# The seven-product FFN kernel: its zone moved by 64 bytes, and the A12 product made fourth of seven

## The chip, the cores and the metric

The kernel runs on one core of one Trainium2 chip. The metric is device time in microseconds (us); the median of the runs is the kernel's time. TensorE is called PE, ScalarE ACT, VectorE DVE, GpSimd POOL and SyncE SP, as in the profile.

## What is computed

A trunk of two layers over 256 rows of 2048 float32 values. Layer 0 has gated linear attention as its mixer, layer 1 attention over 64 selected keys. After each mixer comes a SwiGLU of width 5632, and this is the part that the change touches:

```python
def swiglu(h, w1, w3, w2):
    return (jax.nn.silu(h @ w1) * (h @ w3)) @ w2

for i in range(DEPTH):                      # DEPTH = 2, D_MODEL = 2048, SEQ = 256
    h = rmsnorm(x, norm_mix[i])
    x = x + (gla_mixer(h, ...) if i % 2 == 0 else dsa_mixer(h, ...))
    x = x + swiglu(rmsnorm(x, norm_ffn[i]), ffn_w1[i], ffn_w3[i], ffn_w2[i])
return rmsnorm(x, norm_final)
```

Every weight is read once from HBM in float32.

## The kernel before

**One product.** Weights come in as tiles `raw` of 128 x 4 x 512 float32 (1 MB), loaded by SP. ACT copies a tile to `wh` in the format that PE multiplies fast (L136, in the function `split_w`), and DVE subtracts to get the rest, `wl` (L137). The activations are split in the same way into a high and a low tile. Three matmuls (high by `wh`, high by `wl`, low by `wh`) make one product at nearly full accuracy. The moving operand is always the weight tile, 512 columns; the stationary operand is a 128 x 128 block of the activations. There are four `raw` buffers and three each of `wh` and `wl`.

**The FFN.** `ffn` goes through 11 blocks of 512 hidden columns. Blocks 0, 1, 3, 5, 7 and 9 run `plain`: for w1 and for w3 four groups of 24 matmuls (L464). Blocks 2, 4, 6, 8 and 10 run `pair`, which gets both products of a block, for two halves of the rows, with seven half-sized products instead of eight, by sums of activations (the forms A11, F5, F3, F6, F7, A12, N22 of the normed x) and of weights. A product in `pair` is 24 matmuls (L394) on two chunks of weights. There are two layers, so 10 pairs, with 7 products each, and 12 plain blocks.

**The sums of weights.** `va` and `vb` are the upper halves of w1 and w3, two tiles each. A11 uses `va`, then DVE adds `vb` to it (`plus`, L406). F5 uses the sum, and each of its chunks, once split, gets the lower half of w3 added by a DMA on POOL's queue that accumulates in SBUF (`plus_dma`, L409). F3 uses the lower half of w3, `vc`, loaded through `raw` (L381), and DVE adds it to `vb`. F6 uses `va`, and then a second pair of accumulating DMAs adds the lower half of w1. F7 uses `vb`, A12 the lower half of w1, `vd`, loaded through `raw`, and N22 uses `va`.

**The pieces.** `pair` and `plain` are generators. At each `yield`, `ffn` runs one piece of `pieces`: the down product of two finished blocks, 24 matmuls with one `raw` tile (L483, L490 to L492). The stationary operand there is a tile `g` of finished hidden values. A pair has eight `yield`s, and two blocks make eight pieces, so that pieces and products alternate. `side` holds transposes and their evacuation (`split_t`, L216 to L219), of which a step is taken by `tick` in the middle of products and pieces.

**The order.** The order on each engine follows the program's, with loads moved ahead where their buffer is free: SP issues the loads of the next pair's `va` while the plain block before it runs. On each queue instructions run in order, and one that waits holds up those behind it.

**Where tiles lie.** Pools are allocated one after the other along a partition. `res` holds x and the four tiles `g`, `wp` holds `raw`, `wh` and `wl`, `cm` and `sm` small things. Behind them lies a zone that four pools use in turn: `gp` and `dp` for the mixers (with the normed activations `hh` and `hl`, stationary operands of `gemm`, L202 to L204), `fz0` and `fz1` for the FFNs (with the forms `fh` and `fl`, and `v0`, `v1`, `v2`, `s1`, `y`, `w`). Two tiles named `pad` are never used; they move what is allocated after them. `x`, `g`, `raw`, `wh`, `wl` and the zone begin at these bytes of a partition in the program as built: 3072, 19456, 52224, 84992, 109568 and 140736.

Of the kernel before, what the change touches and what calls it, by code (L numbers as in the profile page):

```python
# [12 lines left out]
F32 = mybir.dt.float32  # L13
# [6 lines left out]
P = 128  # L20
# [35 lines left out]
def trunk(  # L56
# [7 lines left out]
    nc = tc.nc  # L64
# [5 lines left out]
    sm = ctx.enter_context(tc.tile_pool(name="sm", bufs=2))  # L70
# [24 lines left out]
    cols = cst.tile([P, 72], F32, name="cols")  # L95


    sm.tile([P, 24], F32, tag="pad", bufs=1, name="pad")

    def gains(c0, srcs):  # L100

# [14 lines left out]
    def tick():  # L116

        while side:
            try:
                return next(side[0])  # L120
            except StopIteration:
                side.popleft()
# [9 lines left out]
    def split_w(raw, pool=wp):  # L132

        wh = pool.tile([P, 4, NB], F32R, tag="wh", bufs=3 if pool is wp else 1, name="wh")
        wl = pool.tile([P, 4, NB], F32R, tag="wl", bufs=3 if pool is wp else 1, name="wl")
        nc.scalar.copy(wh, raw)  # L136
        nc.vector.tensor_sub(wl, raw, wh.bitcast(F32))  # L137
        return wh, wl
# [230 lines left out]
    def pair(nrm, wa, wb, c0, turn, done):  # L369

        def src(w, j, c):
            r = j * 1024 + c * 512
            return w[r:r + 512, c0:c0 + NB].rearrange("(k p) n -> p k n", p=P)

        def load(w, j, homes):
            o = []
            for c, (pool, tag, bufs) in enumerate(homes):
                raw = pool.tile([P, 4, NB], F32, tag=tag, bufs=bufs, name=tag)  # L380
                nc.sync.dma_start(raw, src(w, j, c))  # L381
                o.append(raw)
            return o

        def product(acc, raws, form, start, stop, then=None):
            for c in range(2):
                wh, wl = split_w(raws[c])
                if then is not None:
                    then(c)
                hi, lo = nrm.forms[form]  # L390
                for j in range(4):
                    k = 4 * c + j
                    for i, (l_, r_) in enumerate(((hi, wh), (hi, wl), (lo, wh))):
                        nc.tensor.matmul(acc, l_[:, k, :], r_[:, j, :], start=start and k == i == 0,  # L394
                                         stop=stop and k == 7 and i == 2, skip_group_check=not start)
                    if j % 2:
                        tick()

        def bank():
            return acc_p.tile([P, NB], F32, tag="acc", name="acc")  # L400

        def sums(tag):
            return nrm.pool.tile([P, NB], F32, tag=tag, bufs=1, name=tag)

        def plus(dst, other):
            return lambda c: nc.vector.tensor_add(dst[c], dst[c], other[c])  # L406

        def plus_dma(dst, w, j):
            return lambda c: nc.gpsimd.dma_start(dst[c], src(w, j, c), accum_op=ALU.add)  # L409

        fz = nrm.pool
        stream = [(wp, "raw", RAW)] * 2
        homes = [((fz, "v0", 1), (fz, "v1", 1)), ((fz, "v2", 1), (res, "g3", 1))]
        va = load(wa, 0, homes[turn])
        vb = load(wb, 0, homes[1 - turn])
        b1 = bank()
        product(b1, va, "A11", True, True, plus(va, vb))
        s1 = sums("s1")
        nc.scalar.copy(s1, b1)
        yield  # L420
        b2 = bank()
        product(b2, va, "F5", True, True, plus_dma(va, wb, 1))
        y = sums("y")
        nc.vector.tensor_sub(y, b2, s1)
        yield
        vc = load(wb, 1, stream)
        product(b2, vc, "F3", False, True, plus(vb, vc))
        yield
        b3 = bank()
        product(b3, va, "F6", True, True, plus_dma(va, wa, 1))  # L430
        w = sums("w")
        nc.vector.tensor_sub(w, b3, s1)
        yield
        product(b3, vb, "F7", False, True)
        nc.vector.tensor_add(w, w, b2)
        nc.vector.tensor_add(y, y, b3)
        yield
        vd = load(wa, 1, stream)
        product(b1, vd, "A12", False, True)
        done("11", b1)  # L440
        done("12", w)
        yield
        product(b3, va, "N22", False, True)
        nc.vector.tensor_sub(s1, s1, b3)
        done("21", s1)
        done("22", y)
        yield
        yield

    def plain(nrm, ws, c0, done):  # L450
# [49 lines left out]
    def ffn(layer, nrm):  # L500
# [5 lines left out]
        for b in range(DFF // NB):  # L506
            us = [None] * NT

            def done(q, v):
                t = int(q[0]) - 1  # L510
                if q[1] == "1":
                    us[t] = cm.tile([P, NB], F32, tag="u", name="u")
                    nc.scalar.activation(us[t], v, AF.Silu, scale=sc["r"][:, t:t + 1])
                else:
                    nc.vector.scalar_tensor_tensor(us[t], us[t], sc["r"][:, t:t + 1], v, op0=ALU.mult, op1=ALU.mult)

            for slot, _ in enumerate(pair(nrm, w1, w3, b * NB, b // 2 % 2, done) if b in range(2, 11, 2) else plain(nrm, (w1, w3), b * NB, done)):
                if b == 0 and slot == 0:
                    flush()
                    r = nrm.rstd()  # L520
                    sc["r"] = r
                while down:
                    try:
                        next(down[0])
                        break
                    except StopIteration:
                        down.popleft()
            hi, lo = hi_lo(b % 3)
            side.append(split_t(us, hi, lo))
            parts.append((hi, lo, b * NB))  # L530
            if b % 2:
                down.append(pieces(w2, parts))
                parts = []
# [560 lines left out]
```

## Time and profile before

| | |
|---|---|
| median of 3 runs | 2283.49 us |
| lowest and highest | 2281.22 and 2284.84 us |
| the profiled execution's own time | 2283.89 us |
| its span | 2282.1 us |
| busy: PE, weight loads, DVE, ACT, POOL | 2254.4, 1856.3, 1499.3, 1127.5, 79.3 us |
| mean granted clock of PE | 0.998 |
| read from HBM | 464.43 MB, 204 GB/s over the span |

The span is the time from the first to the last instruction of the profiled execution. Matmuls overlap, and the end of each is modelled, so PE shows as busy nearly all the time; what a matmul costs is read from one start to the next. A row of the timeline gives the start, the duration, the engine, the line, the operation, output and inputs, and in brackets how long the engine was idle before it and what ended that.

### The profile page before, as it was taken

The page shows a single profiled execution, that of the slowest core. Times are in us where ns is not written, and L with a number is a line of the kernel's source. Part 1 is how long each engine was busy: PE and PEld are TensorE (multiplying, and loading weights), DVE is VectorE, ACT ScalarE, POOL GpSimd, SP SyncE. Part 2 cuts the span into 40 slices and gives each one's busy share as a digit, 9 for nine tenths or more (in the row PEclk, how much of TensorE's full clock was granted, in tenths as well). Part 3 has the DMA queues.
Part 4 walks back from the last instruction along what each step waited for, and adds up shares of the span by engine and source line. Part 5 has one row for each costly group of instructions (what it writes and reads, how often), then busy time and mean ns, then how long its engine had stood idle before and what let it go on. Part 6 is the DMA issues. An engine that isn't in the chain of part 4 may idle for free.

```text
span 2282.1 us, 25208 instructions
## 1 busy us (share of the span) xinstructions
PE 2254.4 (99%) x10343; PEld 1856.3 (81%) x10343; DVE 1499.3 (66%) x1254; ACT 1127.5 (49%) x1026; POOL 79.3 (3%) x131
## 2 busy tenths in 40 slices
PE   9999999999999999999999999999999999999998
PEld 7888888887888888887888888888888788888886
DVE  6546456577676867776655755556675867777676
ACT  5545355444454545545544544455454454545454
POOL 0000000000000000000100000000000000000000
PEclk9999999999999999999999999999999999999999
DMA  8555465759495876857554555457496786949593
GB/s 286 168 171 188 127 233 187 237 160 302 147 299 199 216 263 184 289 159 218 173 182 148 184 166 166 165 186 240 147 277 234 193 273 174 296 146 305 166 239 111
DMA packets 242098, 468.18 MB, mean 205 GB/s; under 512 B 7816, under 2 KB 20448, under 8 KB 241856
## 3 DMA queue, kind: packets, MB, share of 16 engines
q1 hardware_dynamic: 219856, 423.33, 54.4%
q0 software_dynamic: 21120, 41.95, 10.7%
q8 instruction: 81, 1.33, 0.2%
q10 hardware_dynamic: 1008, 1.31, 0.2%
q14 instruction: 33, 0.27, 0.0%
HBM read 464.43 MB, written 2.12 MB: 204 GB/s over the span
## 4 chain that ended last, share of the span: by engine, by line
PE 68%; issue 20%; DMA 5%; DVE 4%; ACT 2%; POOL 0%; POOLq 0%; ACTq 0%; SPq 0%
PE acc L464 14%; PE acc L204 11%; PE acc L202 11%; PE acc L203 11%; PE acc L394 8%; PE down L490 3%; PE down L491 3%; DMA g<-in_ffn_w 3%; PE down L492 3%; DVE wl L137 2%; DMA v<-in_ffn_w 2%; ACT wh L136 1%; DVE v L406 1%; PE tr L216 1%; PE trq L825 0%
## 5 line engine op out<-in xcount | busy, mean ns | idle before, releaser
L137 DVE TENSOR_TENSOR wl<-raw,wh 128x2048 fp32r<-128x2048 f32 x217 | 496.8, 2290 | 261.3 <-ACT wh L136 261.3
L136 ACT CAST wh<-raw 128x2048 fp32r<-128x2048 f32 x217 | 415.7, 1915 | 474.1 <-PE down L492 176.6
L193 DVE TENSOR_TENSOR wl<-raw,wh 128x2048 fp32r<-128x2048 f32 (+3 forms) x147 | 317.8, 2164 | 276.4 <-ACT wh L192 276.3
L192 ACT CAST wh<-raw 128x2048 fp32r<-128x2048 f32 (+3 forms) x147 | 265.5, 1809 | 230.8 <-PE acc L204 194.6
L202 PE MATMUL acc<-wh,hh 128*128 128x512 f32 (+3 forms) x832 | 326.8, 393 | 0.0
L204 PE MATMUL acc<-wh,hl 128*128 128x512 f32 (+3 forms) x832 | 318.4, 383 | 0.0
L203 PE MATMUL acc<-wl,hh 128*128 128x512 f32 (+3 forms) x832 | 317.0, 381 | 0.5 <-DVE wl L193 0.5
L491 PE MATMUL down<-wl,g 128*128 128x512 f32 x640 | 249.2, 389 | 0.0
L492 PE MATMUL down<-wh,g 128*128 128x512 f32 x640 | 249.0, 389 | 0.0
L490 PE MATMUL down<-wh,g 128*128 128x512 f32 x640 | 247.5, 389 | 0.0
L137 DVE TENSOR_TENSOR wl<-v,wh 128x2048 fp32r<-128x2048 f32 x72 | 164.3, 2287 | 44.6 <-ACT wh L136 44.6
L136 ACT CAST wh<-v 128x2048 fp32r<-128x2048 f32 x72 | 137.4, 1908 | 97.0 <-PE acc L394 39.2
L203 PEld LDWEIGHTS acc<-wl,hh 128*128 128x128 f32 x832 | 156.6, 188 | 30.3 <-issue 1.7
L204 PEld LDWEIGHTS acc<-wh,hl 128*128 128x128 f32 x832 | 156.2, 188 | 30.6
L202 PEld LDWEIGHTS acc<-wh,hh 128*128 128x128 f32 x832 | 156.4, 188 | 29.0 <-issue 1.9
L464 PE MATMUL acc<-wh,fhA 128*128 128x512 f32 x384 | 152.2, 396 | 0.1
L464 PE MATMUL acc<-wh,flA 128*128 128x512 f32 x384 | 150.4, 392 | 0.0
L464 PE MATMUL acc<-wl,fhA 128*128 128x512 f32 x384 | 149.8, 390 | 0.0
L490 PEld LDWEIGHTS down<-wh,g 128*128 128x128 f32 x640 | 120.1, 188 | 25.5
L491 PEld LDWEIGHTS down<-wl,g 128*128 128x128 f32 x640 | 120.1, 188 | 25.3
L492 PEld LDWEIGHTS down<-wh,g 128*128 128x128 f32 x640 | 120.1, 188 | 25.0
L394 PE MATMUL acc<-wl,fhF 128*128 128x512 f32 x320 | 127.8, 399 | 8.4 <-DVE wl L137 8.4
(281 smaller groups left out, 3617.0 us busy)
## 6 DMA issues: line engine op xcount, KB each, us to landing
raw<-in_ffn_w SPq DMA_DIRECT2D x224, 1024.0 KB, 5.2
raw<-in_dsa_w_in SPq DMA_DIRECT2D x48, 1024.0 KB, 5.0
raw<-in_gla_w_in SPq DMA_DIRECT2D x40, 1024.0 KB, 5.1
v<-in_ffn_w SPq DMA_DIRECT2D x30, 1024.0 KB, 6.9
v<-in_ffn_w POOLq DMA_DIRECT2D x28, 1024.0 KB, 8.9
raw<-in_gla_w_out SPq DMA_DIRECT2D x16, 1024.0 KB, 5.0
raw<-in_dsa_w_out SPq DMA_DIRECT2D x16, 1024.0 KB, 4.9
g<-in_ffn_w POOLq DMA_DIRECT2D x12, 1024.0 KB, 13.7
```

The source lines that it names most:

```text
L136: nc.scalar.copy(wh, raw)
L137: nc.vector.tensor_sub(wl, raw, wh.bitcast(F32))
L192: a = nc.scalar.copy(wh[:, sl, :n], raw[:, sl, :n])
L193: v = nc.vector.tensor_sub(wl[:, sl, :n], raw[:, sl, :n], wh[:, sl, :n].bitcast(F32))
L202: nc.tensor.matmul(acc[t][:, :n], hi[:, k, ts_], wh[:, k, :n], start=start, stop=False)
L203: nc.tensor.matmul(acc[t][:, :n], hi[:, k, ts_], wl[:, k, :n], start=False, stop=False)
L204: nc.tensor.matmul(acc[t][:, :n], lo[:, k, ts_], wh[:, k, :n], start=False, stop=last)
L394: nc.tensor.matmul(acc, l_[:, k, :], r_[:, j, :], start=start and k == i == 0, stop=stop and k == 7 and i == 2, skip_group_check=not start)
L464: nc.tensor.matmul(acc[bank], l_[:, k, :], r_[:, j, :], start=start and k == i == 0, stop=stop and k == 7 and i == 2, skip_group_check=not ...
L490: nc.tensor.matmul(acc[t], hi[:, k, ts_], wh[:, k, :], start=start, stop=False)
L491: nc.tensor.matmul(acc[t], hi[:, k, ts_], wl[:, k, :], start=False, stop=False)
L492: nc.tensor.matmul(acc[t], lo[:, k, ts_], wh[:, k, :], start=False, stop=last)
```

## The change

Two things. The unused tile `pad` in `sm` grows from 24 to 40 floats per partition. And in `pair`, the product A12 with its loads and its first `done` stands between F3 and F6 instead of between F7 and N22; the sum `w` is finished right after F6; and of the last two `yield`s one now follows F7, so that their number stays.

```diff
-    sm.tile([P, 24], F32, tag="pad", bufs=1, name="pad")
+    sm.tile([P, 40], F32, tag="pad", bufs=1, name="pad")
...
         product(b2, vc, "F3", False, True, plus(vb, vc))
         yield
+        vd = load(wa, 1, stream)
+        product(b1, vd, "A12", False, True)
+        done("11", b1)
+        yield
         b3 = bank()
         product(b3, va, "F6", True, True, plus_dma(va, wa, 1))
         w = sums("w")
         nc.vector.tensor_sub(w, b3, s1)
+        nc.vector.tensor_add(w, w, b2)
+        done("12", w)
         yield
         product(b3, vb, "F7", False, True)
-        nc.vector.tensor_add(w, w, b2)
         nc.vector.tensor_add(y, y, b3)
         yield
-        vd = load(wa, 1, stream)
-        product(b1, vd, "A12", False, True)
-        done("11", b1)
-        done("12", w)
         yield
         product(b3, va, "N22", False, True)
         nc.vector.tensor_sub(s1, s1, b3)
         done("21", s1)
         done("22", y)
-        yield
         yield
```

## Rows read from the trace of the kernel before

**Rows 1.** The page, part 1: busy us, share of the span, instructions.
```profile
PE 2254.4 (99%) x10343; PEld 1856.3 (81%) x10343; DVE 1499.3 (66%) x1254; ACT 1127.5 (49%) x1026; POOL 79.3 (3%) x131
```
**Rows 2.** Waits: who waited for whom; us in total, times, longest us.
```profile
PEld acc L394 <- DVE wl L137: 12.5, 10, 2.1
```
**Rows 3.** Timeline of PE, first pair: starts of F5, a piece, F3.
```profile
497.37 0.39 PE L394 MATMUL acc<-wh,fhF 128*128 128x512 f32 x1
...
502.86 0.39 PE L490 MATMUL down<-wh,g 128*128 128x512 f32 x1
...
508.30 0.39 PE L394 MATMUL acc<-wh,fhF 128*128 128x512 f32 x1
```
**Rows 4.** Timeline of PE, first pair: F6's start, its second half, the piece.
```profile
519.23 0.39 PE L394 MATMUL acc<-wh,fhF 128*128 128x512 f32 x1
...
523.77 0.51 PE L394 MATMUL acc<-wl,fhF 128*128 128x512 f32 x1 [1.39 <-DVE wl L137]
...
526.42 0.39 PE L490 MATMUL down<-wh,g 128*128 128x512 f32 x1
```
**Rows 5.** Timeline of PE, last pair: starts of F6 and of the piece.
```profile
2197.09 0.39 PE L394 MATMUL acc<-wh,fhF 128*128 128x512 f32 x1
...
2203.66 0.40 PE L490 MATMUL down<-wh,g 128*128 128x512 f32 x1
```
**Rows 6.** Fifth pair: the same two starts, then windows (busy us, PEclk, DMA share, GB/s).
```profile
1034.06 0.39 PE L394 MATMUL acc<-wh,fhF 128*128 128x512 f32 x1
...
1043.62 0.40 PE L490 MATMUL down<-wh,g 128*128 128x512 f32 x1
...
1034.10:1043.60 9.50, 7.56 (x25) 5.53 (x24) 6.53 (x3) 5.51 (x3) 1.29 (x1) 0.82 0.91 200
```
**Rows 7.** Timeline of ACT and DVE: the split of F6's second chunk, first pair.
```profile
519.47 1.92 ACT L136 CAST wh<-g 128x2048 fp32r<-128x2048 f32 x1 [6.31 <-PE down L492]
...
521.42 2.29 DVE L137 TENSOR_TENSOR wl<-g,wh 128x2048 fp32r<-128x2048 f32 x1 [5.94 <-ACT wh L136]
```
**Rows 8.** Timeline of POOL, first pair; the middle row: the first's KB, us to landing.
```profile
505.38 1.31 POOL L409 DMA_DIRECT2D g<-in_ffn_w  x1 [7.72 <-DVE y L424]
...
g<-in_ffn_w POOLq DMA_DIRECT2D x1, 1024.0 KB, 14.0
...
519.63 1.29 POOL L409 DMA_DIRECT2D v<-in_ffn_w  x1 [12.94 <-DMA g<-in_ffn_w]
```
**Rows 9.** DMA issues at 507.42 (first pair) and 1022.25 (fifth): KB, us to landing.
```profile
raw<-in_ffn_w SPq DMA_DIRECT2D x1, 1024.0 KB, 12.5
...
raw<-in_ffn_w SPq DMA_DIRECT2D x1, 1024.0 KB, 13.3
```
**Rows 10.** Timeline, first pair: the piece behind N22 (PE), the last `u` (DVE).
```profile
559.23 0.39 PE L490 MATMUL down<-wh,g 128*128 128x512 f32 x1
...
563.64 0.74 DVE L515 SCALAR_TENSOR_TENSOR u<-u,rstd,y 128x512 f32<-128x512 f32 x1
```
**Rows 11.** PE in `gemm`: starts with `g`, with `hh`; groups by line: count | busy, mean ns.
```profile
1094.37 0.39 PE L202 MATMUL acc<-wh,g 128*128 128x512 f32 x1
...
1096.41 0.39 PE L202 MATMUL acc<-wh,g 128*128 128x512 f32 x1
...
1155.69 0.39 PE L202 MATMUL acc<-wh,hh 128*128 128x512 f32 x1
...
1161.18 0.39 PE L202 MATMUL acc<-wh,hh 128*128 128x512 f32 x1
...
L202 PE MATMUL acc<-wh,hh 128*128 128x512 f32 x736 | 296.5, 403 | 0.0
```
**Rows 12.** Timeline of PE in a plain block, 24 matmuls apart.
```profile
1609.83 0.39 PE L464 MATMUL acc<-wh,fhA 128*128 128x512 f32 x1
...
1615.33 0.39 PE L464 MATMUL acc<-wh,fhA 128*128 128x512 f32 x1
```
**Rows 13.** The page, part 6: DMA issues; count, KB each, median us to landing.
```profile
raw<-in_ffn_w SPq DMA_DIRECT2D x224, 1024.0 KB, 5.2
```

## The prediction, made before the changed kernel was run

> **What bounds the kernel now.** I read the page first: TensorE (PE) is busy for 2254.4 us, 99% of the span [rows 1], so any change has to act on PE, either on its idle time or on the time from one matmul to the next. Then the waits of PE: in the loop of `pair` the one large entry is weight loads of L394 that wait for VectorE's `wl` of L137, 12.5 us in 10 times [rows 2], once in each of the 10 pairs. Then the timeline of PE in a pair. Seven products and the pieces (of `down`, one at each `yield`) alternate. An undisturbed product of 24 matmuls, F5, takes 502.86 − 497.37 = 5.49 us and the piece behind it 508.30 − 502.86 = 5.44 us [rows 3]. The fourth product, F6, takes 526.42 − 519.23 = 7.19 us in the first pair: its second half begins with a matmul on `wl` at 523.77 [rows 4]. In the last pair it takes 2203.66 − 2197.09 = 6.57 us [rows 5]. In the fifth it takes 1043.62 − 1034.06 = 9.56 us, and there the granted clock of the stretch is 0.82 [rows 6]: PE idled, and ran several matmuls at the lower of its two levels (1.2 GHz, not 2.4) afterwards. Read in the same way, from F6's first row to the piece's first row, the ten F6 (first, fifth and last shown) take 7.19, 6.18, 6.38, 5.77, 9.56, 6.96, 7.00, 5.70, 6.85 and 6.57, in sum 68.16 us. Ten undisturbed products would take 54.9, so F6 loses **13.2 us**.
>
> **Why F6 waits.** ScalarE casts the second half of `va` (tile g3) at 519.47, VectorE subtracts at 521.42, and with its 2.29 us it is done at 523.7, when PE goes on [rows 7, 4]. The cast is late because g3 is being added to by DMA: that transfer was issued on POOL at 505.38 and took 14.0 us, so it landed at 519.4, and the next one on POOL starts only behind it, at 519.63 [rows 8]. The first half's transfer had kept POOL's next issue until 505.38. Between F5 (which frees `va`) and F6 there stand only a piece, F3 and a piece, 16.4 us; two such transfers in a row don't fit.
>
> **The change, part by part. 1: A12 between F3 and F6.** F6 now begins one product and one piece later, 5.49 + 5.44 = 10.9 us, near 530.2 in the first pair. Its second half needs the landing by F6's start + 2.75 (half a product) − 1.92 − 2.29 [rows 7], that is by 528.7; it lands near 519.4, 9.3 us early. Even a transfer 5 us slower than the shown one is hidden. So the 13.2 us go, the price of the low clock in the fifth pair with them. No instruction is added or removed: A12's 24 matmuls, its two loads, its two casts and subtractions and `done("11")` move, and one of the two `yield`s at the end moves ahead of N22, so that the pieces stay eight.
>
> What is late next? Four things move nearer to their users.
> (a) The loads. On SP the two `raw` loads of A12 pass the loads of two pieces. The four `raw` buffers are refilled in order, so the fourth load of this stretch, issued at 507.4 and landed 12.5 us later at 519.9 [rows 9], is today A12's first half, not wanted for two products yet, and becomes the piece behind A12, which PE reaches at 524.7. Cast and subtraction need it by 520.6 at the latest: 0.7 us to spare. In the fifth pair it is issued at 1022.25 and takes 13.3 us [rows 9], 1035.5, against a limit of 1035.5: nothing to spare. Loads issued behind it can't hold it up by much, as they follow it in SP's own queue. I price this at 0 to 1 us a pair, and 0.5 us in all, because the first pair's row still has spare time.
> (b) N22 needs the second pair of adding DMAs, which start when F6 has split `va`. F6 to N22 was piece, F7, piece, A12, piece; it is now piece, F7, two pieces: 5.5 us less. The first is issued near 526 to 527; if both took 14.0 us [rows 8] they would land at 555, and N22's second half (PE near 560.1) needs it by 555.9. Price nothing; the cover is the two pieces, and without one of them it would cost up to 5 us a pair.
> (c) Behind N22 one piece stands instead of two. The chain to the last `u` ended at 563.64 + 0.74 = 564.4, 5.2 us after N22's end at 559.23 [rows 10]. The transposes that read it come after one piece and two steps of the next block, 5.4 + 1.4 us. Hidden by 1.6 us; at the two ends of the FFNs, where they follow the piece at once, by 0.2 us.
> (d) `w`: both its operations now follow F6, 1.4 us of VectorE with a piece of 5.4 us ahead of F7, which writes the same bank. `done("11")` waits on ScalarE for A12's end, with F6's second cast behind it, as N22's second cast stood behind it before. Nothing.
>
> **2: the 64 bytes.** The pad in `sm` grows from 96 to 160 bytes, so the rest of `sm` and all that is allocated behind it move by 64: the zone pools `gp`, `fz0`, `dp`, `fz1`. As the program is laid out, the zone begins at byte 140736 of a partition, 448 past a multiple of 512, and the stationary tiles in it (`hh`, `hl`, `fh`, `fl`), being multiples of 2048 long, all begin there too. The `g` tiles in `res` begin at multiples of 512, as do `raw`, `wh` and `wl`; these don't move. Afterwards the zone begins at 140800, a multiple of 512. What may this be worth? A product (stationary operand in the zone) takes 5.49 us for 24 matmuls, 228.8 ns each; a piece (stationary operand in `g`, same moving tiles, same moment) takes 5.44, 226.7 ns [rows 3]. The same two rates show on the same lines of `gemm`: with `hh` 1161.18 − 1155.69 = 5.49 us for 24, with `g` 1096.41 − 1094.37 = 2.04 for 9, that is 226.7 ns [rows 11]. A plain block has 1615.33 − 1609.83 = 5.50 for 24 [rows 12]. So matmuls that differ in nothing but where the stationary tile lies differ by 2.2 ns. Their number: 10 pairs x 7 x 24 = 1680; 12 plain blocks x 2 x 4 x 24 = 2304; in `gemm` 3 x 736 = 2208 [rows 11]; in all 6192. If the place within 512 bytes is the cause, 6192 x 2.2 = 13.6 us go; matmuls beside a transpose need not gain, and I take **13 us**. The bounds are 0 and 13.6. Below zero: some tiles in `dp` behind the small `rb` (queries, `cth`) leave multiples of 128 for 64 past them; if those some 500 matmuls lost the same 2.2 ns it would cost 1.1 us. The long casts of `v` (in the zone) and `raw` (not) gave no reason to expect ScalarE or VectorE to change, and they are not the bound.
>
> That the place decides is an inference, as the `g` tiles also lie lower in SBUF than everything in the zone. The Trainium skill, SBUF — State Buffer, Specifications (TRN2), gives lines of 16 bytes, and says that crossing into a new line costs; 140736 and 140800 are both multiples of 16, so by that rule the move would bring nothing. The 2.2 ns in the rows are not explained by that rule; what it would make of the time is the first rival.
>
> **Sum.** Profiled run 2283.89 us (span 2282.1 and 1.8 around it): 2283.9 − 13.2 − 13.0 + 0.5 = 2258.2. The median of the runs shown, 2283.49, is 0.4 below the profiled one, so I say **2258 us**, and 2254 to 2263 if this case holds.
>
> **Rivals.** *The 64 bytes do nothing*: the 2.2 ns come from the tiles lying high, not from their place within 512 bytes. Against it stands that all stationary tiles of the zone, from its first to its last byte, show one rate. Time: 2283.5 − 13.2 + 0.5 = 2271. *The wait only moves*: the load of (a) lands 2 us later than in the rows, the piece behind A12 waits 1.3 us in each pair, 13 us, and only the bytes count: 2283.5 − 13 = 2271 as well (2284 if they do nothing either). *Slower*: SP's queue has one more load ahead of that piece's. A load takes 5.2 us in the median [rows 13], so it would land near 525, 4.4 us past its limit, in each of 10 pairs, 44 us: 2258 + 44 = 2302. It decides from about 2.6 us past the limit, where the 26 us are used up; the fifth pair's clock shows that such waits also cost a stretch at half speed. For it: the DMA share of that stretch is 0.91 [rows 6]. Against it: only the order of the loads changes, not their number, and each is issued when a buffer comes free.
>
> **Chances.** Forecast 0.68 (2258); bytes nothing 0.18 (2271); wait moves 0.05 (2271); both, no change, 0.03 (2284); slower 0.06 (2302). A measurement of this kernel can tell about 0.2%, 4.6 us. Faster 0.91, same 0.03, slower 0.06. The range takes in the first three cases with their bounds, 2253 to 2273.
>
> **What would show it.** F6 at 5.5 us or less in all ten pairs, no `wl` wait of L394, and a granted clock of 1.00 where the fifth pair had 0.82, show part 1; a longer piece behind A12 shows the moved wait. Products, plain blocks and `gemm` on `hh` at 5.44 us for 24 show part 2; at 5.49 it does nothing. The prediction is wrong if the scheduler orders the loads otherwise, or if the rate follows the height in SBUF.

## The result, and the profile after

The changed kernel takes 2264.34 us in the median of 4 runs (2263.56 to 2265.86), against 2282.65 for the kernel before in the same comparison: a ratio of 0.9917, interval 0.9905 to 0.9929. It is 18.3 us faster. The prediction was 2258, some 25 us faster. The profiled execution took 2265.86 us, its span is 2264.1.

The page after, its first lines: the span, and part 1, which answers to [rows 1].

```profile
span 2264.1 us, 25200 instructions
PE 2243.0 (99%) x10343; PEld 1852.8 (82%) x10343; DVE 1501.4 (66%) x1254; ACT 1128.1 (50%) x1026; POOL 79.4 (4%) x131
```

PE is the bound as before, and the other engines are as busy as they were. What PE's weight loads waited for (total us, times, longest), which answers to [rows 2]:

```profile
PEld down L491 <- DVE wl L137: 4.5, 7, 1.7
...
PEld down L490 <- DVE x L497: 3.7, 15, 0.3
```

The line of [rows 2], L394 on `wl`, is gone: no product waits any more. In its place two lines of pieces stand that the kernel before did not have. The timeline of PE in the first pair shows both sides. These are the starts of F5, a piece, F3, a piece, A12, the piece behind it and its second matmul, F6, and the next piece:

```profile
495.79 0.39 PE L394 MATMUL acc<-wh,fhF 128*128 128x512 f32 x1
...
501.23 0.39 PE L490 MATMUL down<-wh,g 128*128 128x512 f32 x1
...
506.67 0.39 PE L394 MATMUL acc<-wh,fhF 128*128 128x512 f32 x1
...
512.11 0.39 PE L490 MATMUL down<-wh,g 128*128 128x512 f32 x1
...
517.55 0.39 PE L394 MATMUL acc<-wh,fhA 128*128 128x512 f32 x1
...
522.99 0.39 PE L490 MATMUL down<-wh,g 128*128 128x512 f32 x1
523.76 0.50 PE L491 MATMUL down<-wl,g 128*128 128x512 f32 x1 [0.38 <-DVE wl L137]
...
529.12 0.39 PE L394 MATMUL acc<-wh,fhF 128*128 128x512 f32 x1
...
534.57 0.39 PE L490 MATMUL down<-wh,g 128*128 128x512 f32 x1
```

F5 takes 501.23 − 495.79 = 5.44 us, where [rows 3] have 5.49, and so does F3. F6 takes 534.57 − 529.12 = 5.45, where [rows 4] have 7.19. The piece behind A12 takes 529.12 − 522.99 = 6.13 where an undisturbed one takes 5.44. In the fifth pair F6 starts at 1040.49, and its window (length, then PE, PEld, DVE, ACT and POOL busy, PEclk, DMA share, GB/s) answers to the last line of [rows 6]:

```profile
1040.50:1045.90 5.40, 5.40 (x25) 4.50 (x24) 3.71 (x4) 3.83 (x2) 0.00 (x0) 1.00 1.03 183
```

The granted clock is 1.00 there, where it was 0.82. Two rows of a plain block 24 matmuls apart answer to [rows 12], and two of `gemm` with `hh` to the 5.49 us of [rows 11]:

```profile
1604.38 0.39 PE L464 MATMUL acc<-wh,fhA 128*128 128x512 f32 x1
...
1609.82 0.39 PE L464 MATMUL acc<-wh,fhA 128*128 128x512 f32 x1
...
1143.74 0.39 PE L202 MATMUL acc<-wh,hh 128*128 128x512 f32 x1
...
1149.18 0.39 PE L202 MATMUL acc<-wh,hh 128*128 128x512 f32 x1
```

Both are 5.44 us for 24, as predicted if the place counts.

**Where the time went.** To add it up, every time from one matmul's start to the next one's is put down to the line of the first, over the whole trace. That gives, in us, for the kernels of this document (gemm is L202 to L204, products L394, plain L464, pieces L490 to L492; for the experiments, the same lines where they have moved):

| kernel | products | plain | gemm | pieces | span |
|---|---|---|---|---|---|
| before | 400.8 | 530.5 | 776.2 | 435.7 | 2282.1 |
| after | 384.6 | 526.0 | 773.7 | 440.6 | 2264.1 |
| e1_bytes | 407.4 | 526.0 | 775.2 | 435.8 | 2284.1 |
| e2_order | 387.9 | 530.6 | 776.6 | 437.4 | 2270.9 |
| e3_g_off | 395.8 | 530.6 | 781.1 | 447.6 | 2294.2 |
| e4_piece_later | 384.6 | 526.0 | 773.6 | 437.6 | 2261.2 |
| e5_at128 | 393.8 | 538.1 | 783.0 | 438.2 | 2291.7 |
| e6_at256 | 384.6 | 526.0 | 773.5 | 438.9 | 2262.7 |
| e7_forms_moved | 384.6 | 526.0 | 776.9 | 437.2 | 2265.0 |
| e8_v_moved | 387.9 | 530.6 | 773.6 | 438.7 | 2269.1 |
| e9_before_v_off | 397.4 | 526.0 | 773.7 | 435.4 | 2272.0 |
| e10_later_v_off | 384.6 | 526.0 | 773.6 | 437.8 | 2261.0 |
| e11_after_v_off | 384.6 | 526.0 | 773.5 | 437.0 | 2260.1 |

From before to after: products −16.2, plain −4.5, gemm −2.5, pieces +4.9; the rest, some 140 us of other work, is 0.3 us longer. The first three are the prediction's two parts. The pieces are what it missed.

### The profile page after: what moved, and what is told of

Read it like the earlier page. It is cut to its first block, busy times and chain, and to the rows that moved or that the text cites. A ratio compares the mean times of both kernels' runs of the same rounds, so it can differ in the third digit from the quotient of the medians.

```text
span 2264.1 us, 25200 instructions
## 1 busy us (share of the span) xinstructions
PE 2243.0 (99%) x10343; PEld 1852.8 (82%) x10343; DVE 1501.4 (66%) x1254; ACT 1128.1 (50%) x1026; POOL 79.4 (4%) x131
## 4 chain that ended last, share of the span: by engine, by line
PE 91%; DVE 3%; DMA 3%; ACT 2%; issue 1%; SPq 0%; POOL 0%; ACTq 0%; POOLq 0%
PE acc L464 22%; PE acc L394 14%; PE acc L204 11%; PE acc L202 11%; PE acc L203 11%; PE down L491 6%; PE down L490 6%; PE down L492 6%; DMA raw<-in_ffn_w 2%; DVE wl L137 1%; PE tr L216 1%; ACT wh L136 1%; DVE wl L193 1%; PE trq L825 0%; PE po L684 0%
## 5 line engine op out<-in xcount | busy, mean ns | idle before, releaser
L202 PE MATMUL acc<-wh,hh 128*128 128x512 f32 (+3 forms) x832 | 325.5, 391 | 0.0
L204 PE MATMUL acc<-wh,hl 128*128 128x512 f32 (+3 forms) x832 | 317.4, 381 | 0.0
L492 PE MATMUL down<-wh,g 128*128 128x512 f32 x640 | 249.2, 389 | 0.0
L490 PE MATMUL down<-wh,g 128*128 128x512 f32 x640 | 248.6, 391 | 0.0
L204 PEld LDWEIGHTS acc<-wh,hl 128*128 128x128 f32 x832 | 156.3, 188 | 29.4
L202 PEld LDWEIGHTS acc<-wh,hh 128*128 128x128 f32 x832 | 156.5, 188 | 28.5 <-issue 1.9
L464 PE MATMUL acc<-wh,fhA 128*128 128x512 f32 x384 | 150.8, 393 | 0.2
L464 PE MATMUL acc<-wl,fhA 128*128 128x512 f32 x384 | 149.6, 390 | 0.0
L464 PE MATMUL acc<-wh,flA 128*128 128x512 f32 x384 | 149.6, 390 | 0.0
L490 PEld LDWEIGHTS down<-wh,g 128*128 128x128 f32 x640 | 120.1, 188 | 29.0 <-DVE x L497 3.7
L492 PEld LDWEIGHTS down<-wh,g 128*128 128x128 f32 x640 | 120.2, 188 | 24.4
L202 PE MATMUL acc<-wh,g 128*128 128x512 f32 x312 | 123.3, 395 | 2.8 <-ACT g L218 2.8
```

The costliest lines, as they stand in the source:

```text
L202: nc.tensor.matmul(acc[t][:, :n], hi[:, k, ts_], wh[:, k, :n], start=start, stop=False)
L204: nc.tensor.matmul(acc[t][:, :n], lo[:, k, ts_], wh[:, k, :n], start=False, stop=last)
L464: nc.tensor.matmul(acc[bank], l_[:, k, :], r_[:, j, :], start=start and k == i == 0, stop=stop and k == 7 and i == 2, skip_group_check=not ...
L490: nc.tensor.matmul(acc[t], hi[:, k, ts_], wh[:, k, :], start=start, stop=False)
L492: nc.tensor.matmul(acc[t], lo[:, k, ts_], wh[:, k, :], start=False, stop=last)
```

## Experiments: the two parts, alone and with one thing changed

All eleven kernels compute the whole reference. Times are medians; the ratio is to the kernel before on the same chip, with its 95% interval.

**e1_bytes: the 64 bytes without the new order.**

```diff
-    sm.tile([P, 24], F32, tag="pad", bufs=1, name="pad")
+    sm.tile([P, 40], F32, tag="pad", bufs=1, name="pad")
```

> The order of before with the pad of 40 floats, so only the zone moves by 64 bytes. In the changed kernel the time between PE starts fell by 4.5 us in plain blocks, 2.5 us in gemm, and from 5.49 to 5.44 us per undisturbed product (70 of them, 3.8 us). If the parts add up, this kernel is 10.8 us faster than before, 2271.9 us, with F6 still waiting 13.2 us in sum. Rival: PE reaches F6 sooner while the adding DMAs land as late as ever, so part of the gain is given back there, up to 0.3 us in each of 10 pairs: 2275 us, with F6 waiting about 16 us. If the place of the zone does nothing by itself: 2282.7 us.

Measured: 2289.16 us (2283.26 to 2294.94), ratio 1.0018 [1.0008, 1.0029]. By itself the move gives nothing; it even costs a little, which none of the three cases of the expectation had. Yet the rates did change: plain blocks fall from 530.5 to 526.0 us, and every product but F6 and A11 takes 5.44. The gain is gone at F6, whose ten take 77.6 us instead of 68.2. The seventh pair is the worst. PE's rows are F6's start, the first four matmuls of its second half, and the next piece; the last line is the window of that half:

```profile
1807.92 0.39 PE L394 MATMUL acc<-wh,fhF 128*128 128x512 f32 x1
...
1811.02 0.50 PE L394 MATMUL acc<-wh,fhF 128*128 128x512 f32 x1 [0.21 <-ACT wh L136]
1813.34 0.80 PE L394 MATMUL acc<-wl,fhF 128*128 128x512 f32 x1 [1.82 <-DVE wl L137]
1813.93 0.63 PE L394 MATMUL acc<-wh,flF 128*128 128x512 f32 x1
1814.36 0.63 PE L394 MATMUL acc<-wh,fhF 128*128 128x512 f32 x1
...
1817.39 0.39 PE L490 MATMUL down<-wh,g 128*128 128x512 f32 x1
...
1811.00:1817.40 6.40, 4.56 (x13) 3.45 (x14) 6.40 (x3) 3.56 (x2) 0.00 (x0) 0.73 1.00 172
```

F6 takes 9.47 us. PE waits for ScalarE and then for VectorE, and the granted clock of the second half is 0.73: the matmuls from 1813.93 to 1816.07 follow each other after 0.43 us, the lower of the two levels. Why F6 waits longer than before, while nothing was moved in the order, is a question that e7 to e9 take up.

**e2_order: the new order without the 64 bytes.** The diff of `pair`, with `pad` left at 24.

> The order of after with the pad of 24 floats, so only A12 moves. F6 should lose its 13.2 us, products stay at 5.49 us, and the piece behind A12 should wait as in the changed kernel or a little less (3.2 us in sum there), since PE gets to it some 0.2 us later: 10 us faster than before, 2272.6 us. Rival: the order is worth its full 13.2 us and the waits of that piece come from the faster PE alone: 2269.5 us and no wait there.

Measured: 2272.98 us (2272.27 to 2274.02), ratio 0.9946 [0.9934, 0.9958]. A12, the piece, F6 and the next piece in the first pair:

```profile
519.30 0.39 PE L394 MATMUL acc<-wh,fhA 128*128 128x512 f32 x1
...
524.79 0.39 PE L490 MATMUL down<-wh,g 128*128 128x512 f32 x1
...
530.23 0.39 PE L394 MATMUL acc<-wh,fhF 128*128 128x512 f32 x1
...
535.73 0.39 PE L490 MATMUL down<-wh,g 128*128 128x512 f32 x1
```

Products stay at 5.49 to 5.50, F6 waits for nothing, and the piece behind A12 takes 5.44: the order alone removes F6's wait, and moves it hardly anywhere (pieces +1.7 us, and one wait of 0.4 us in the eighth pair). It is worth some 12 us, with 13.2 less about 0.5 predicted. The theory of this expectation, that the piece behind A12 waits as in the changed kernel, was wrong; its rival was right about the wait.

**The parts don't add.** The bytes alone cost 4 us or so, the order alone gains 12, both gain 18. With the old order what the bytes give is lost at F6; with the new one most of it is kept.

**e3_g_off: is it the place within 512 bytes, or the height in SBUF?** The tiles `g` are moved to 64 past a multiple of 512, and the zone stays 448 past one, in the order of before.

```diff
+    res.tile([P, 16], F32, tag="gpad", name="gpad")
...
+    res.tile([P, 112], F32, tag="gpad2", name="gpad2")
```

> Before, with the g tiles moved by 64 bytes (to 64 past a multiple of 512) and all that lies behind them by 512, so that the moving tiles and the zone keep their places within 512 bytes. If the place within 512 bytes sets the rate, pieces go from 5.44 to 5.49 us for 24 matmuls (1920 matmuls) and gemm on g as well (936): 5 to 6 us slower, 2288 us. If it is the height of the zone in SBUF that sets the rate, pieces stay at 5.44 us and the time at 2282.7 us.

Measured: 2296.66 us (2295.36 to 2300.43), ratio 1.0052 [1.0036, 1.0067]. A piece and the start of the next product, first pair (lines are one further on in this kernel):

```profile
505.57 0.39 PE L491 MATMUL down<-wh,g 128*128 128x512 f32 x1
...
511.17 0.40 PE L395 MATMUL acc<-wh,fhF 128*128 128x512 f32 x1
```

5.60 us for 24, or 233.2 ns, where `g` at a multiple of 512 gave 226.7 [rows 3]. The tiles lie as low as before and are slower than the zone's: it is the place and not the height. The direction is as expected, the size is twice the 5 to 6 us. The sum closes: pieces grow by 11.9 us (1920 × 6.2 ns) and `gemm` on `g` by 4.9 (936 × 5.2), against F6, whose ten take 61.0 us, 7.1 less. PE reaches F6 0.6 us later in a pair, which leaves the transfers more time. `g3`, a target of those transfers, moved too, but the second adding DMA lands 33.3 us after the start of A11 where it landed at 33.4. That is 9.7 of the 12.1 us by which the span grew. One thing does not fit: 18 of the 53 undisturbed products after A11 take 5.60 instead of 5.50 us, though their stationary tiles did not change their place within 512 bytes (the products but F6 grow by 2.1 us, most of the rest of the sum). That is left open.

**e5_at128 and e6_at256: which places are good?** The changed kernel, with the zone at 128 and at 256 past a multiple of 512.

```diff
-    sm.tile([P, 40], F32, tag="pad", bufs=1, name="pad")
+    sm.tile([P, 72], F32, tag="pad", bufs=1, name="pad")     (e6: 104)
```

> The changed kernel with a pad of 72 floats, so the zone begins 128 bytes past a multiple of 512. If a multiple of 128 is enough, products take 5.44 us and the time is that of the changed kernel, 2264 us. If 512 is wanted, products take 5.49 us or more (the kernel with g at 64 past a multiple took 5.60 us per piece) and the time is 2273 us or more.

> The changed kernel with a pad of 104 floats: the zone begins 256 bytes past a multiple of 512. With 128 or 256 enough: products of 5.44 us, 2264 us. With 512 wanted: 5.49 us or more, 2273 us or more.

Measured: at 128, 2294.17 us, ratio 1.0050 [1.0035, 1.0065]; at 256, 2266.79 us, ratio 0.9931 [0.9914, 0.9948]. F5 and the piece behind it in the first pair, at 128 (first three rows) and then a product and the piece's start at 256:

```profile
502.97 0.40 PE L394 MATMUL acc<-wh,fhF 128*128 128x512 f32 x1
...
508.56 0.39 PE L490 MATMUL down<-wh,g 128*128 128x512 f32 x1
...
514.02 0.40 PE L394 MATMUL acc<-wh,fhF 128*128 128x512 f32 x1
```

```profile
507.12 0.39 PE L394 MATMUL acc<-wh,fhF 128*128 128x512 f32 x1
...
512.55 0.39 PE L490 MATMUL down<-wh,g 128*128 128x512 f32 x1
```

At 128 a product takes 5.59 us, at 256 5.43, as good as a multiple of 512. So a multiple of 256 is enough, and one of 128 is not. The kernel at 128 has the new order and is still 11 us slower than before: a place can cost more than the order gains.

## Experiments: who is late in the new order

**What is late.** The third pair of the changed kernel has the longest wait. The rows: the piece behind A12 and its second matmul on PE, F6's start, then the cast on ACT and the subtraction on DVE of that piece's weights, and last the DMA issue at 761.52 that loads them (KB, us to landing):

```profile
778.68 0.39 PE L490 MATMUL down<-wh,g 128*128 128x512 f32 x1
780.36 0.50 PE L491 MATMUL down<-wl,g 128*128 128x512 f32 x1 [1.29 <-DVE wl L137]
...
785.75 0.39 PE L394 MATMUL acc<-wh,fhF 128*128 128x512 f32 x1
...
776.07 1.91 ACT L136 CAST wh<-raw 128x2048 fp32r<-128x2048 f32 x1 [4.33 <-DMA raw<-in_ffn_w]
...
778.02 2.29 DVE L137 TENSOR_TENSOR wl<-raw,wh 128x2048 fp32r<-128x2048 f32 x1 [3.95 <-ACT wh L136]
...
raw<-in_ffn_w SPq DMA_DIRECT2D x1, 1024.0 KB, 14.5
```

This is the load of step (a). It lands at 761.5 + 14.5 = 776.0; cast and subtraction follow at once, and PE goes on at 780.36. The piece takes 785.75 − 778.68 = 7.07 us. In the ten pairs it takes 6.13, 5.85, 7.07, 5.44, 5.61, 5.44, 5.47, 5.98, 5.44 and 5.69, in sum 3.7 us more than ten undisturbed ones. The order alone (e2) hardly shows this, with the same loads in the same order: only its eighth pair has 5.69, the other nine 5.44.

**e4_piece_later: take the waiting piece away.** The changed kernel, with the piece behind A12 moved behind F6: A12 and F6 run one after the other, and the `yield`s stay eight.

```diff
         product(b1, vd, "A12", False, True)
         done("11", b1)
-        yield
         b3 = bank()
...
         done("12", w)
         yield
+        yield
```

> The changed kernel without the piece between A12 and F6; it runs behind F6, so two pieces stand there. Theory: the piece behind A12 waits for its weights, whose load lands up to 2.7 us into A12; with F6 ahead of it that load has 5.4 us more, and the 3.2 us of waits go: 2261 us. F6 begins 5.4 us sooner, and its adding DMA, which landed 1.6 to 2.5 us into A12, has to be there 4.0 us into A12, so F6 waits nowhere. Rival: the wait moves once more, to F6 or to the first of the two pieces: 2264 us.

Measured: 2263.10 us (2262.93 to 2264.76), ratio 0.9904 [0.9889, 0.9918]. A12, F6 and the piece behind F6, first pair:

```profile
517.81 0.39 PE L394 MATMUL acc<-wh,fhA 128*128 128x512 f32 x1
...
523.25 0.39 PE L394 MATMUL acc<-wh,fhF 128*128 128x512 f32 x1
...
528.69 0.39 PE L490 MATMUL down<-wh,g 128*128 128x512 f32 x1
```

Both products take 5.44 us, and no line of waits for `wl` is left. Pieces fall from 440.6 to 437.6 us, and the profiled span by 2.9. In the medians this is 1.2 us, and the two intervals overlap: the wait is real in the trace, and its removal is hardly more than a measurement can tell. The time lies between the theory's 2261 and the rival's 2264.

**e7_forms_moved and e8_v_moved: what made the load late?** Two things moved by 64 bytes that may matter here: the stationary tiles (PE became faster, so all is wanted sooner), and `v0`, `v1`, `v2`, into which DMAs load and add. In e7 the FFN's stationary tiles lie at a multiple of 512 and the `v` tiles 448 past one; in e8 it is the other way round. Both have the new order.

```diff
+            for q in ("v0", "v1", "v2"):
+                pool.tile([P, 4, NB], F32, tag=q, bufs=1, name=q)
+            pool.tile([P, 16], F32, tag="fpad", bufs=1, name="fpad")    (e7, pad 24)
+            pool.tile([P, 112], F32, tag="fpad", bufs=1, name="fpad")   (e8, pad 40)
```

> The changed kernel, but in the FFN zones v0, v1 and v2 come first and stay at 448 past a multiple of 512, while the forms (and s1, y, w) lie at a multiple of 512; hh and hl of the mixers stay at 448. In the four kernels with the pad of 40 the fourth load of a pair landed 34.8 to 35.1 us after the pair's start on the mean, with the pad of 24 at 34.1 to 34.2. Theory: where the v tiles lie, into which the adding DMAs go, sets how long transfers take side by side; then it lands at 34.2 here, and the piece behind A12 hardly waits: products 5.44 us, 2264 us, gemm 2.5 us slower and the waits 2.5 us less. Rival: the faster matmuls of PE are what slows the transfers; then it lands at 35.0 and the piece waits 3 us in sum, 2267 us.

> The mirror of the one before: v0, v1, v2 (and hh, hl) at a multiple of 512, the forms at 448 past one. Products and plain blocks at 5.49 and 5.50 us for 24. If the v tiles' place slows the transfers, the fourth load lands at 35.0 us, but PE comes later too, so the piece waits little: 2272 us. If PE's rate does, it lands at 34.2 and nothing waits: 2270 us. The landing tells them apart, the time hardly.

Measured: e7 2265.49 us, ratio 0.9925 [0.991, 0.994]; e8 2271.88 us, ratio 0.9952 [0.9937, 0.9967]. The same load of the third pair as above, in e7 and then in e8 (DMA issues at 763.49 and 762.32):

```profile
raw<-in_ffn_w SPq DMA_DIRECT2D x1, 1024.0 KB, 12.3
```

```profile
raw<-in_ffn_w SPq DMA_DIRECT2D x1, 1024.0 KB, 13.5
```

The faster PE of e7 does not make the load late; the `v` tiles at a multiple of 512 do, even beside the slower PE of e8. Over the ten pairs, from the first matmul of A11 to the landing of the second adding DMA and of that load:

| `v` tiles lie at | kernels | second adding DMA, us | the load, us |
|---|---|---|---|
| 448 past a multiple of 512 | before, e2, e3, e7 | 33.3 to 33.6 | 34.1 to 34.2 |
| 64 past | e9, e10, e11 | 33.4 to 33.5 | 34.0 to 34.1 |
| 128 past | e5 | 32.9 | 33.8 |
| a multiple of 256 | e1, after, e4, e6, e8 | 34.2 to 34.8 | 34.8 to 35.1 |

At a multiple of 256 these transfers land some 0.8 us later, whatever the order and whatever PE's rate. Step (a)'s limit, counted in the same way, is 520.6 − 485.5 = 35.1: on average the load was 0.9 us ahead of it before, and is 0.1 us ahead after.

**e9, e10 and e11: good place for the stationary tiles, `v` tiles at 64 past.** In all three the `v` tiles lie between two small pads, with `pad` at 40. e9 has the order of before, e11 that of after, e10 that of e4.

```diff
+            pool.tile([P, 16], F32, tag="fpad", bufs=1, name="fpad")
+            for q in ("v0", "v1", "v2"):
+                pool.tile([P, 4, NB], F32, tag=q, bufs=1, name=q)
+            pool.tile([P, 48], F32, tag="fpad2", bufs=1, name="fpad2")
```

> The order of before, hh, hl and the forms at multiples of 256, v0 to v2 at 64 past one. The kernel with only the pad changed had all of them at multiples of 512; its matmuls took 10.8 us less outside F6, but F6's waits grew from 13.2 to 23.2 us. Theory: the growth comes from the v tiles' place, which makes the second adding DMA land at 34.2 instead of 33.4 us after the pair's start; here it lands at 33.4 again, F6 waits 13 to 14 us and the time is 2272 to 2273 us. Rival: F6 waits more because PE gets there with faster matmuls and the low clock follows each long wait; then F6 still waits over 20 us and the time stays near 2284 us.

> The kernel without a piece between A12 and F6, with v0 to v2 at 64 past a multiple of 512 and everything stationary at a multiple of 256. There no wait was left in the pairs that a quicker transfer could shorten, so by the theory the time stays at 2263 us; if transfers still cost something that the list of waits does not show, it falls below 2261 us.

> The changed kernel with v0 to v2 at 64 past a multiple of 512. By the theory the fourth load of a pair lands at 34.1 instead of 35.0 us after its start, the piece behind A12 waits under 1 us in sum instead of 3.2, and the time is 2262 us. By the rival (PE's rate slows the transfers) it stays at 2264 us with the same waits.

Measured: e9 2276.76 us (2273.74 to 2281.81), ratio 0.9973 [0.9959, 0.9987]; e10 2262.73 us (2262.49 to 2263.18), ratio 0.9912 [0.9899, 0.9926]; e11 2263.60 us (2261.87 to 2265.03), ratio 0.9915 [0.9902, 0.9929]. PE's waits in e1 and then in e9 (there the product is at L398), the same order with the `v` tiles moved off the multiple of 256 (the forms behind them move too, from one multiple of 256 to another):

```profile
PEld acc L394 <- DVE wl L137: 19.3, 10, 2.1
```

```profile
PEld acc L398 <- DVE wl L137: 14.1, 10, 2.1
```

In e9 the ten F6 take 67.5 us, 13.1 more than ten undisturbed products of 5.44 (13.2 in the kernel before), against 77.6 in e1: the 10 us that e1 lost at F6 hang on the `v` tiles' place. Of these, 0.76 us later landings in ten pairs are 7.6; in the sixth and seventh pair of e1 six matmuls each step at 0.43 us instead of 0.23, which is an estimated 2.4 more and makes up the rest. With that out of the way the bytes alone gain 10 us in the profiled run (span 2272.0), which is the fastest of the seven, and 6 to 8 by the ratio and the medians, even in the old order. The median lies between the theory's 2272 to 2273 and the rival's 2284; it is F6's rows that decide for the theory.

In e11 no piece waits for `wl` any more, the load of the third pair takes this long,

```profile
raw<-in_ffn_w SPq DMA_DIRECT2D x1, 1024.0 KB, 12.2
```

and the pieces take 437.0 us. Its profiled span is 4.0 us below that of after. The median is only 0.7 below, within the uncertainty: the profiled run of after, 2265.86, is the slowest of its four, so its waits are likely on the high side of them. e10, both remedies at once, has the lowest median of all kernels here and the narrowest spread; by the ratio e4 is lower still (0.9904 against 0.9912), so the two are alike. e10 is 0.9% faster than the kernel before, and 1.6 us below after, less than the two intervals can tell apart.

## Why the prediction was right, and where it was not

The direction, the place of the gain and the mechanism of both parts held, and 2264.3 is within the range, but above the 2254 to 2263 of the forecast's own case: the number is in the range because the range took in the two rivals at 2271. By its own steps:

- **F6's wait, −13.2: right.** All ten F6 take 5.44 to 5.45 us; the half-speed stretch of the fifth pair went with the wait, as said. e2 shows it by itself, at 5.50.
- **The 64 bytes, −13.0: the cause was right, the size too large.** They gave some 3.0 in products (16.2 − 13.2), 4.5 in plain blocks and 2.5 in `gemm`, 10.0 in all. e3 and e5 settle that the place decides, and not the height; a multiple of 256 is as good as the 512 of the prediction (e6). The mis-sized term is `gemm`: 2208 matmuls were priced at the full 2.2 ns but gained 2.5 us, 1.1 ns each. The prediction allowed that "matmuls beside a transpose need not gain", and took off 0.6 us for it. Rows of after, starts of every third matmul of `gemm` behind a transpose:

```profile
1134.94 0.48 PE L202 MATMUL acc<-wh,hh 128*128 128x512 f32 x1
...
1135.72 0.40 PE L202 MATMUL acc<-wh,hh 128*128 128x512 f32 x1
...
1136.41 0.40 PE L202 MATMUL acc<-wh,hh 128*128 128x512 f32 x1
...
1137.11 0.39 PE L202 MATMUL acc<-wh,hh 128*128 128x512 f32 x1
```

Three matmuls take 0.78, 0.69 and 0.70 us, and 0.68 in undisturbed stretches (5.44 / 8). The slower pace outlasts the interruption by several matmuls, and in `gemm` other work of PE stands close together. Of the 2208 steps, 689 are among the first eight behind such an interruption, and these took 0.2 us more after than before; the other 1519 took 2.7 us less. The 1.1 us that the prediction allowed for tiles in `dp` did not come: all other work of PE takes 125.8 us before and 125.9 after.
- **The new waits, +0.5: this step failed.** The pieces grew by 4.9 us. Some 3.7 are the piece behind A12, the place that step (a) named, in 7 of 10 pairs; the rival "the wait only moves" was at work at a quarter of its price. The limit was right, and so was the load's landing as long as the `v` tiles keep their old place (e2, e7). What failed is that (a) took the load's duration from the kernel before and costed part 2 for PE alone: it looked for a change in ScalarE and VectorE from the `v` tiles' place, and not in the DMAs that write them. That made the load 0.8 us later, as much as the step had to spare. "Only the order of the loads changes" was true, and not enough.
- **(b), N22: no wait, as said, but not free.** Two pieces in a row now stand ahead of N22, and the program as scheduled puts N22's first matmul ahead of the second of them:

```profile
550.88 0.39 PE L394 MATMUL acc<-wh,fhN 128*128 128x512 f32 x1
551.15 0.50 PE L490 MATMUL down<-wh,g 128*128 128x512 f32 x1
...
556.74 0.39 PE L394 MATMUL acc<-wl,fhN 128*128 128x512 f32 x1
```

That piece takes 556.74 − 551.15 = 5.59 us, 0.15 more than an undisturbed one, some 1.5 us in ten pairs. It stands with the waits for `x` of L497, the sum that takes up the first piece's result, in the second line of the waits above. It was priced at nothing, and e7 and e11, whose pieces are 1.3 to 1.5 us above before with no wait for `wl`, show it alone.
- **(c) and (d): right.** F7 waits for nothing. The weight loads of transposes wait for `u` 2.7 us in all, at most 0.3 a time, but no wait of PE itself goes with it. And this is not the order's doing: e1, with the old order, has the same 2.7, and e2, with the new one, 0.6.

So −13.2 − 10.0 + 4.9 + 0.3 is the −18.0 of the spans, where −25.7 was forecast: 3.0 are missing in the bytes' term, and 4.4 in the waits'. Of the rivals, that the bytes do nothing fell with e3; its time, 2271, is near what e2 measured without them. The slower rival was on the right load. Its price, a whole transfer of 5.2 us, never came; delays of up to 1.6 us did.

## What to carry to other kernels

When a tile moves, price every reader and writer of every tile that moves with it, the DMAs too: here the stationary tiles gained and the DMA targets lost, and parting them kept the gain without the loss. A term read from the old trace, such as a load's landing, holds only while nothing in the change touches what the load runs beside; with 0.7 us to spare and a second part that moves the buffers, the spare time belongs in the range. And two parts that meet at one wait are measured each alone before their gains are added: the same 64 bytes cost 4 us with one order and give some 7 with the other.

## What the runs showed of the hardware

The pace of matmuls in this form (float32 data in the fast format, 512 columns, a weight load for each) hangs on the place of the stationary tile. Undisturbed, with the place counted modulo 256 bytes: 226.7 ns at 0, 233.2 at 64 (e3), 232 to 233 at 128 (e5), 228.8 to 229 at 192 (before, e2, e8). That places 256 bytes apart are alike was tried for 0 only (after and e6). The Trainium skill, SBUF — State Buffer, Specifications (TRN2), gives lines of 16 bytes with a penalty for each crossing; all four places are multiples of 16, and the measured paces differ by up to 6.5 ns, so here that rule does not tell which place is good. Why 128 is worse than 192, and why some products of e3 took on the pace of the pieces beside them, is open.

The loads that run beside the adding DMAs land some 0.8 us later (34.8 to 35.1 us against 33.8 to 34.2) where the `v` tiles lie at a multiple of 256. In the traces the casts and subtractions of `v` take 1.91 and 2.29 us at either place, and the packets of the adding DMAs 183 to 186 ns; those of SP's load queue, from 10 to 35 us behind the start of A11, take 91 to 92 ns on the mean with the `v` tiles at a multiple of 256 and 86 to 88 elsewhere. Which access to the `v` tiles slows them, the DMAs that load or add to these tiles or the reads of ScalarE and VectorE, was not tried.

Kernels with F6's wait also vary more from run to run: 17 runs of before and 12 of e1 spread over some 12 us each, the six, five and four runs of e2, e4 and e10 over 1 or 2. The traces show the lower clock behind some of these waits (fifth pair of before, sixth and seventh of e1), so how much they cost is not the wait alone; that this makes the spread is likely, but was not shown.
